# Norms of a diffusion block: squares added in another order, root transposed from one column, transposed root read in PSUM

## The chip, the cores and the metric

The kernel runs on one core of one Trainium2 chip. The metric is the device time of one execution in microseconds (us). The engines are TensorE (PE, with its weight loads PEld), VectorE (DVE), ScalarE (ACT), GpSimd (POOL) and SyncE (SP); DMAs move data between the chip's memory and the on-chip memory SBUF. TensorE writes its results to PSUM, a second on-chip memory of eight banks.

## What is computed

Two layers over 512 latent tokens and 256 context tokens, each token with 1024 features. Layer 0 is attention, layer 1 a Mamba-2 scan (SSD); a gated feed-forward block with a convolution (ConvFFN) follows each. Each sub-layer begins with the same norm:

```python
def rms_norm(x, g):
    xf = x.astype(jnp.float32)
    y = xf * lax.rsqrt(jnp.mean(xf * xf, axis=-1, keepdims=True) + EPS)
    return (y * g.astype(jnp.float32)).astype(x.dtype)

def modulate(x, shift, scale):
    return x * (1 + scale) + shift

for i in range(DEPTH):                       # DEPTH = 2
    h_l = modulate(rms_norm(x, norm_mix_w[i]), mod_l[0], mod_l[1])
    h_c = modulate(rms_norm(ctx, norm_mix_w[i]), mod_c[0], mod_c[1])
    # attention (i = 0) or SSD (i = 1), then x += mod_l[2] * o_l and, for i = 0, ctx += mod_c[2] * o_c
    h_l = modulate(rms_norm(x, norm_ffn_w[i]), mod_l[3], mod_l[4])
    x = x + mod_l[5] * conv_ffn(h_l, ffn_w_up[i], ffn_conv_w[i], ffn_conv_b[i], ffn_w_down[i])
    # the same for ctx when i = 0
```

## The kernel before, in words

Activations lie transposed: a tile is 128 features by up to 512 tokens, and eight tiles (m = 0 to 7) hold the 1024 features. Every large product is made of three matmuls: weights and activations are split into a high part in a shorter number format (fp32r) and a low part, the rest (`wh` and `wl`, `hh` and `hl`). ScalarE casts the high part of a weight, VectorE subtracts to get `wl` (line 87).

A norm needs, for every token, the sum of squares over all features, that is over the partitions of eight tiles. The steps are these:

- `Norm.sq`: as each tile m of the stream x is finished (line 781, VectorE, `X<-ps_d`), ScalarE squares it (line 325). GpSimd adds the squares of tiles 1 to 5 onto that of tile 0. The squares of tiles 6 and 7 are added to each other on VectorE (line 330), and then that sum and the first one (line 332), also on VectorE.
- `rstd_rows`: TensorE sums over the partitions, with the squares as weights and a column of ones (`ss`, line 236); this gives one column per 128 tokens with the tokens on the partitions. VectorE scales it (`rsa`, line 239), ScalarE takes Ln and Exp (line 241, `rsy`), VectorE refines by one Newton step (`rsu`, lines 243 and 244). The last step of it (line 247) writes the root `rb` 128 columns wide, the same value in each, and TensorE transposes it (`rsT`, line 253), so that it lies in PSUM with the tokens along the columns, the same on every partition.
- `Norm.gen`: ScalarE copies `rsT` to SBUF as `rs` (line 345). `modulated` then makes the eight tiles `h`: VectorE multiplies x by the gain and the root (`ht`, line 281), ScalarE adds the shift and writes the high part (line 290, or lines 286 and 287), and VectorE (line 291) or GpSimd (line 288) writes the low part.

`rstd_rows` serves other norms too: the norm `a` ahead of attention, the norm `y` inside the SSD mixer, and the norm `q` of queries and keys, which has two column groups (`cols` of two columns, so c = 2); all others have c = 1.

The class Norm is used three times: f0 (ahead of layer 0's ConvFFN), s (ahead of the SSD mixer) and f1 (ahead of layer 1's ConvFFN). f0 and s have three segments of 256 tokens: the context, then the two halves of the latents; f1 has the two latent halves. While the product ahead of the norm (`down`, tiles `ps_d`, or `ps_wo` for f1) goes on for one segment, the norm of the segment before it runs beside it, one step for every tile m. Behind the product stand the first two output tiles of the next one (`first_tiles`, tiles `ps_first`), segment by segment. They need the `h` of their segment and hide the norm of the segments after it.

PSUM is given out as two double banks (`S`, for `ps_first`) and four single banks:

```python
def Bank(g, name):
    return g.ps.tile([P, 512], F32, tag="B", bufs=4, name=name)
```

`ps_d`, `ps_wo`, `ss` and `rsT` all take one of these four while they live. SBUF tiles such as `rb`, `rs`, `ht` and `sq` come from one pool of equal buffers (`t3`).

The order of instructions on every engine is fixed when the program is built: a planner goes through the program in the order written, with a cost for each instruction, and moves forward what it takes to be ready sooner. On the chip each engine runs its own list in order, and semaphores make it wait for others.

Of the kernel before, what the change touches and what calls it, by code (L numbers as in the profile page):

```python
# [7 lines left out]
P = 128  # L8
# [3 lines left out]
ALU = mybir.AluOpType  # L12
# [55 lines left out]
def t3(g, name, dt=F32, n=T):  # L68
    return g.t3p.tile([P, n], dt, tag="t3", bufs=g.n3, name=name)
# [106 lines left out]
class Fill:  # L176
# [6 lines left out]
    def add(self, gen):  # L183
        self.q.append(gen)
# [17 lines left out]
    def require(self, gen):  # L202
        for _ in gen:
            pass
        if gen in self.q:
            self.q.remove(gen)
# [8 lines left out]
def follow(g, bi):  # L215

    if g.last_act is not None:
        g.tc.add_manual_dep(bi.ins, g.last_act.ins.name, mybir.DependencyInfo(
            mybir.DependencyClass.NoSync, mybir.DependencyReason.DATA), reason="order of tables")
    g.last_act = bi  # L220
# [6 lines left out]
def rstd_rows(g, sq, n, cols, width, name, bank):  # L227

    nc = g.nc
    c = cols.shape[-1]
    nt = n // P
    ps = bank(f"ss{name}")
    for t in range(nt):
        nc.tensor.matmul(ps[:, t * c : (t + 1) * c], sq[:, t * P : (t + 1) * P], cols, start=True, stop=True)
    small = lambda nm: g.p.tile([P, nt * c], F32, tag="rst", bufs=8, name=nm)
    a, y, u = small("rsa"), small("rsy"), small("rsu")
    nc.vector.tensor_scalar(a, ps[:, : nt * c], 1.0 / width, EPS, ALU.mult, ALU.add)

    for f in ((lambda: nc.scalar.activation(y, a, AF.Ln)), (lambda: nc.scalar.activation(y, y, AF.Exp, scale=-0.5))):
        follow(g, f()) if g.tables else f()
    nc.vector.tensor_tensor(u, y, a, ALU.mult)
    nc.vector.scalar_tensor_tensor(u, y, -0.5, u, ALU.mult, ALU.mult)
    rb = t3(g, f"rb{name}", n=n)
    wide = lambda v: v.unsqueeze(2).broadcast_to([P, nt * c, P // c])
    nc.vector.scalar_tensor_tensor(rb.rearrange("p (a b) -> p a b", b=P // c), wide(u), 1.5, wide(y), ALU.add, ALU.mult)
    yield BREAK
    out = []
    for t0 in range(0, nt, 4):  # L250
        pt = bank(f"rsT{name}")
        for t in range(t0, min(nt, t0 + 4)):
            nc.tensor.transpose(pt[:, (t - t0) * P : (t - t0 + 1) * P], rb[:, t * P : (t + 1) * P], g.ident)
        yield (pt, t0 * P, min(n, (t0 + 4) * P))


def parts(x, a=0, b=1 << 30):


    x = x if isinstance(x, list) else [x]  # L260
    out, c = [], 0
    for ap in x:
        n = ap.shape[-1]
        lo, hi = max(a, c), min(b, c + n)
        if lo < hi:
            out.append((ap[:, lo - c : hi - c], lo - a, hi - a))
        c += n
    return out
# [6 lines left out]
def modulated(g, hl, x, rs, a, b, layer, ca, cb, v, m, pool=False):  # L275

    nc = g.nc
    n = b - a
    t = t3(g, "ht", n=n)
    for ap, c0, c1 in parts(x[m], a, b):  # L280
        nc.vector.scalar_tensor_tensor(t[:, c0:c1], ap, g.moda[layer][ca][:, m, v : v + 1], rs[:, c0:c1],  # L281
                                       ALU.mult, ALU.mult)
    bias = g.mod[layer][cb][:, m, v : v + 1]
    hi, lo = (h[:, a:b] for h in hl)
    if pool:
        nc.scalar.activation(t, t, AF.Identity, bias=bias)
        nc.scalar.copy(hi, t)
        nc.gpsimd.tensor_tensor(lo, t, _r(hi), ALU.subtract)
        return
    nc.scalar.activation(hi, t, AF.Identity, bias=bias)  # L290
    nc.vector.scalar_tensor_tensor(lo, t, bias, _r(hi), ALU.add, ALU.subtract)
# [14 lines left out]
def Bank(g, name):  # L306
    return g.ps.tile([P, 512], F32, tag="B", bufs=4, name=name)


class Norm:  # L310
# [8 lines left out]
    def sq(self, seg, x, m):  # L319

        i, a, b = seg
        nc = self.g.nc
        sq = t3(self.g, f"sq{self.name}", n=b - a)
        for ap, c0, c1 in parts(x[i][m], a, b):
            nc.scalar.activation(sq[:, c0:c1], ap, AF.Square)
        if m in (0, 6):
            self.acc[seg, m] = sq
            return
        acc = self.acc[seg, 6 if m == 7 else 0]
        (nc.vector if m == 7 else nc.gpsimd).tensor_tensor(acc, acc, sq, ALU.add)  # L330
        if m == 7:
            nc.vector.tensor_tensor(acc, acc, self.acc[seg, 0], ALU.add)

    def gen(self, seg, x, lag=2):

        i, a, b = seg
        g, nc, n = self.g, self.g.nc, b - a
        for _ in range(lag):
            yield
        rows = rstd_rows(g, self.acc[seg, 6], n, g.ones[:, :1], D, self.name, lambda nm: Bank(g, nm))  # L340
        next(rows)
        for _ in range(lag):
            yield
        rs = t3(g, f"rs{self.name}", n=n)
        nc.scalar.copy(rs, next(rows)[0][:, :n])
        for m in range(KT):
            modulated(g, self.h[i][m], x[i], rs, a, b, *self.a, self.streams[i][1], m,
                      pool=m in ((1, 4) if a else (1, 3, 5, 7)))
            yield
# [30 lines left out]
def attention(g, fill, X, late):  # L380
# [57 lines left out]
    for m in range(KT):  # L438
        sq = t2("sql") if m else acc
        nc.scalar.activation(sq, xs[0][m], AF.Square)  # L440
        if m:
            nc.vector.tensor_tensor(acc, acc, sq, ALU.add)
    norm = rstd_rows(g, acc, L, g.ones[:, :1], D, "a", Bk)
    g.qn8 = g.const.tile([P, 1], F32, name="qn8")
    nc.vector.tensor_scalar(g.qn8, g.par[:, PC["qn"] : PC["qn"] + 1], HD ** -0.5, None, ALU.mult)
# [23 lines left out]
    for m in range(KT):  # L469
# [11 lines left out]
        if m == 3:  # L481
            norm = rstd_rows(g, sqc, C, g.ones[:, :1], D, "a", Bk)
            next(norm)
# [956 lines left out]
```

## Time and profile before

| | |
|---|---|
| median of 3 runs (lowest to highest) | 1893.8 us (1892.28 to 1894.25) |
| the profiled execution | 1893.6 us, span 1891.8 us |
| TensorE busy | 1859.4 us, 98% of the span |
| VectorE busy | 1314.9 us, 70% |
| ScalarE busy | 811.4 us, 43% |
| GpSimd busy | 302.8 us, 16% |
| granted TensorE clock, mean | 0.997 |

A row of a profile view names the line, the engine, the operation, the tiles written and read (`out<-in`), their shape and how often it was. The view of waits gives the engine and the line that waited, behind the arrow the instruction that released it, and the total in us, the number of waits and the longest. The view in order of time gives the start, the duration, the instruction and, in brackets, the idle time of the engine before it. In the view of one line or tile the three numbers are the smallest, median and largest duration in ns. In the view of stretches each engine has its busy time and, in brackets, its instructions; behind the engines stands the granted TensorE clock.

### The profile page before, as it was taken

The numbers are of one execution on the slowest core, as the hardware profiler recorded it, in microseconds if no ns is written. First come the engines' busy times: TensorE is split into PE (matmuls) and PEld (weight loads), VectorE is DVE, ScalarE is ACT, GpSimd is POOL, SyncE is SP. The second block draws the span as 40 slices with busy tenths as digits, with TensorE's granted clock in tenths as the row PEclk, the third lists the DMA queues.
The fourth block names the chain that finished last, engine by engine and source line by source line (L and its number), as shares of the span: only waits on it lengthen the run. The fifth ranks groups of instructions, "written<-read, shape, count | busy, mean of one in ns | idle before, by whom it ended". The sixth has DMA issues, their size and how long they took to land.

```text
span 1891.8 us, 28789 instructions
## 1 busy us (share of the span) xinstructions
PE 1859.4 (98%) x11474; PEld 1548.3 (82%) x11474; DVE 1314.9 (70%) x1950; ACT 811.4 (43%) x1410; POOL 302.8 (16%) x266
## 2 busy tenths in 40 slices
PE   9999999999999999999999999999999999999999
PEld 7866565688888888888888888888887888888887
DVE  6587778687877776444487877777787476565655
ACT  4544443364222222222366676776666252323331
POOL 2231120040000000000041334444333210000000
PEclk9999999999999999999999999999999999999999
DMA  9322341115443553112224323333453222323232
GB/s 342 91 95 62 132 156 37 34 57 190 145 134 131 180 182 123 65 67 68 67 90 125 114 92 116 118 120 126 123 158 106 72 91 100 100 83 107 90 100 89
DMA packets 74070, 211.67 MB, mean 112 GB/s; under 512 B 9040, under 2 KB 14544, under 8 KB 73808
## 3 DMA queue, kind: packets, MB, share of 16 engines
q1 hardware_dynamic: 73936, 209.84, 33.5%
q8 instruction: 90, 1.47, 0.3%
q14 instruction: 44, 0.36, 0.1%
HBM read 198.79 MB, written 6.82 MB: 109 GB/s over the span
## 4 chain that ended last, share of the span: by engine, by line
PE 80%; DVE 11%; issue 3%; DMA 2%; ACT 2%; POOL 1%; SPq 0%; DVEq 0%; POOLq 0%; ACTq 0%
PE ps_up L108 10%; PE ps_up L106 10%; PE ps_up L105 10%; PE ps_d L105 6%; PE ps_d L106 6%; PE ps_d L108 6%; PE ps_in L108 4%; PE ps_in L106 4%; PE ps_in L105 4%; PE ps_o L636 2%; PE ps_s L672 2%; PE ps_st L1030 2%; DVE ht L281 1%; DVE wl L87 1%; PE ps_wo L108 1%
## 5 line engine op out<-in xcount | busy, mean ns | idle before, releaser
L87 DVE TENSOR_TENSOR wl<-wst,wh 128x1024 fp32r<-128x1024 f32 x207 | 260.4, 1258 | 229.3 <-PE ps_up L106 133.0
L85 ACT CAST wh<-wst 128x1024 fp32r<-128x1024 f32 x211 | 221.1, 1049 | 396.4 <-DMA wst<-in_wup 321.5
L106 PE MATMUL ps_up<-hlf,wh 128*128 128x512 f32 (+1 forms) x1008 | 357.0, 354 | 0.0
L108 PE MATMUL ps_up<-hhf,wl 128*128 128x512 f32 (+1 forms) x1008 | 356.8, 354 | 0.0
L105 PE MATMUL ps_up<-hhf,wh 128*128 128x512 f32 x1008 | 356.8, 354 | 0.0
L106 PEld LDWEIGHTS ps_up<-hlf,wh 128*128 128x128 f32 x1008 | 190.7, 189 | 26.3
L105 PEld LDWEIGHTS ps_up<-hhf,wh 128*128 128x128 f32 x1008 | 190.5, 189 | 26.5
L108 PEld LDWEIGHTS ps_up<-hhf,wl 128*128 128x128 f32 x1008 | 190.5, 189 | 26.3
L105 PE MATMUL ps_in<-hhs,wh 128*128 128x512 f32 (+1 forms) x560 | 204.4, 365 | 1.2 <-ACT dt L915 1.2
L106 PE MATMUL ps_in<-hls,wh 128*128 128x512 f32 (+1 forms) x560 | 199.4, 356 | 0.0
L108 PE MATMUL ps_in<-hhs,wl 128*128 128x512 f32 (+1 forms) x560 | 198.7, 355 | 0.0
L105 PE MATMUL ps_d<-hdh,wh 128*128 128x512 f32 (+1 forms) x568 | 193.5, 342 | 0.2 <-ACT hdh L85 0.2
L108 PE MATMUL ps_d<-hdh,wl 128*128 128x512 f32 (+1 forms) x568 | 193.5, 341 | 0.0
L106 PE MATMUL ps_d<-hdl,wh 128*128 128x512 f32 (+1 forms) x568 | 192.9, 340 | 0.3 <-DVE hdl L87 0.3
L781 DVE SCALAR_TENSOR_TENSOR X<-ps_d,mod,X 128x512 f32<-128x512 f32 (+1 forms) x224 | 124.8, 587 | 35.2 <-PE ps_d L108 35.0
L105 PEld LDWEIGHTS ps_in<-hhs,wh 128*128 128x128 f32 x560 | 105.9, 189 | 16.3 <-ACT dt L915 1.4
L106 PEld LDWEIGHTS ps_d<-hdl,wh 128*128 128x128 f32 x568 | 106.7, 188 | 14.8 <-DVE hdl L87 0.7
L108 PEld LDWEIGHTS ps_in<-hhs,wl 128*128 128x128 f32 x560 | 105.8, 189 | 14.8
L108 PEld LDWEIGHTS ps_d<-hdh,wl 128*128 128x128 f32 x568 | 106.7, 188 | 13.1
L105 PEld LDWEIGHTS ps_d<-hdh,wh 128*128 128x128 f32 x568 | 106.3, 188 | 13.6 <-ACT hdh L85 0.7
L106 PEld LDWEIGHTS ps_in<-hls,wh 128*128 128x128 f32 x560 | 106.0, 189 | 13.2
L675 ACT ACTIVATE pr<-ps_s 128x1024 f32<-128x1024 f32 x56 | 57.2, 1022 | 108.8 <-PE ps_s L674 106.5
(344 smaller groups left out, 3682.8 us busy)
## 6 DMA issues: line engine op xcount, KB each, us to landing
wst<-in_wup SPq DMA_DIRECT2D x88, 512.0 KB, 3.3
wada<-in_adaT SPq DMA_DIRECT2D x56, 512.0 KB, 3.3
wst<-in_win SPq DMA_DIRECT2D x48, 512.0 KB, 3.4
wst<-in_wdown SPq DMA_DIRECT2D x44, 512.0 KB, 3.9
E<-ad SPq DMA_DIRECT2D x64, 256.0 KB, 6.4
wada<-in_adaB SPq DMA_DIRECT2D x24, 512.0 KB, 4.0
ec<-ead SPq DMA_DIRECT2D x64, 128.0 KB, 5.1
wst<-in_wout SPq DMA_DIRECT2D x16, 512.0 KB, 3.3
```

Source lines behind the costliest of these rows:

```text
L85: keep(nc.scalar.copy(hi, src))
L87: keep(eng.tensor_tensor(lo, src, _r(hi), ALU.subtract))
L105: mm(out, wh, ah, start=first, stop=False)
L106: mm(out, wh, al, start=False, stop=False)
L108: mm(out, wl, ah, start=False, stop=last)
L281: nc.vector.scalar_tensor_tensor(t[:, c0:c1], ap, g.moda[layer][ca][:, m, v : v + 1], rs[:, c0:c1], ALU.mult, ALU.mult)
L636: nc.tensor.matmul(po[S64[e], :n], v, pr[:, 512 * e + off : 512 * e + off + n], start=first, stop=last)
L672: nc.tensor.matmul(outs[e], kk[e][a][S64[e], k], b[S64[e], q], start=i == 0, stop=False)
L675: nc.scalar.activation(pr, ps, AF.Exp)
L781: nc.vector.scalar_tensor_tensor(ap, o[:, c0:c1], gate[:, m, v : v + 1], ap, ALU.mult, ALU.add)
L1030: nc.tensor.matmul(ps[:, d * 256 : (d + 1) * 256], Bt[:, t * P : (t + 1) * P], xw[d][t], start=t == ts[0], stop=t == ts[-1])
```

## The change

Three edits. In `rstd_rows`, for c = 1, the last Newton step writes one column per 128 tokens, into the small tile `a`; the transposes read this column as a 128x128 operand with a stride of zero. For c = 2 all stays as it was. In `Norm.sq`, for tile 7, the sum of tiles 0 to 5 is added to the square of tile 6 first, and the square of tile 7 last. In `Norm.gen`, `rs` is no longer a copy: `modulated` reads the transposed root in PSUM. The norms a and y keep their copies (lines 461 and 1220); the norm a already reads PSUM for its first tile (line 459).

```diff
-    rb = t3(g, f"rb{name}", n=n)
-    wide = lambda v: v.unsqueeze(2).broadcast_to([P, nt * c, P // c])
-    nc.vector.scalar_tensor_tensor(rb.rearrange("p (a b) -> p a b", b=P // c), wide(u), 1.5, wide(y), ALU.add, ALU.mult)
+    if c == 1:
+        nc.vector.scalar_tensor_tensor(a, u, 1.5, y, ALU.add, ALU.mult)
+        root = lambda t: a[:, t : t + 1].broadcast_to([P, P])
+    else:
+        rb = t3(g, f"rb{name}", n=n)
+        wide = lambda v: v.unsqueeze(2).broadcast_to([P, nt * c, P // c])
+        nc.vector.scalar_tensor_tensor(rb.rearrange("p (a b) -> p a b", b=P // c), wide(u), 1.5, wide(y),
+                                       ALU.add, ALU.mult)
+        root = lambda t: rb[:, t * P : (t + 1) * P]
     yield BREAK
-    out = []
     for t0 in range(0, nt, 4):
         pt = bank(f"rsT{name}")
         for t in range(t0, min(nt, t0 + 4)):
-            nc.tensor.transpose(pt[:, (t - t0) * P : (t - t0 + 1) * P], rb[:, t * P : (t + 1) * P], g.ident)
+            nc.tensor.transpose(pt[:, (t - t0) * P : (t - t0 + 1) * P], root(t), g.ident)
         yield (pt, t0 * P, min(n, (t0 + 4) * P))
...
         acc = self.acc[seg, 6 if m == 7 else 0]
-        (nc.vector if m == 7 else nc.gpsimd).tensor_tensor(acc, acc, sq, ALU.add)
         if m == 7:
             nc.vector.tensor_tensor(acc, acc, self.acc[seg, 0], ALU.add)
+        (nc.vector if m == 7 else nc.gpsimd).tensor_tensor(acc, acc, sq, ALU.add)
...
-        rs = t3(g, f"rs{self.name}", n=n)
-        nc.scalar.copy(rs, next(rows)[0][:, :n])
+        rs = next(rows)[0][:, :n]
```

## The prediction

> **What bounds the kernel now.** I read the busy times on the page first, then the waits of TensorE in the stretches where the norms stand, then the queues of the other engines in those stretches.
>
> ```profile
> PE 1859.4 (98%) x11474; PEld 1548.3 (82%) x11474; DVE 1314.9 (70%) x1950; ACT 811.4 (43%) x1410; POOL 302.8 (16%) x266
> ```
>
> TensorE is the bound over the whole span, so an edit to the norms can only win back places where TensorE stands idle for them. The next rows are TensorE's waits from 392 to 432 us (norm f0), 950 to 990 us (norm s) and 1470 to 1540 us (norm f1); the columns are the total in us, how often, and the longest.
>
> ```profile
> PE rsTf L253 <- DVE rbf L247: 1.0, 3, 0.4
> PE ps_first L106 <- DVE hlf L291: 0.5, 1, 0.5
> PE ps_first L108 <- DVE wl L87: 0.4, 1, 0.4
> ...
> PE rsTs L253 <- DVE rbs L247: 1.0, 3, 0.4
> PE ps_first L106 <- DVE hls L291: 1.0, 2, 0.6
> PE ps_first L108 <- DVE wl L87: 0.6, 1, 0.6
> ...
> PE ps_first L105 <- ACT hhf L290: 1.5, 1, 1.5
> PE ps_first L106 <- POOL hlf L288: 1.2, 1, 1.2
> PE ps_first L105 <- ACT hhf L287: 0.2, 1, 0.2
> PE ssf L236 <- DVE sqf L332: 0.2, 1, 0.2
> ```
>
> They sum to 7.6 us, of which the 1.0 us for wl (a weight's low part) is no work of the norm. So about 6.6 us, 0.35% of the span, is all that a shorter norm can free in waits. There are two kinds: the transpose rsT stands in TensorE's queue before its root is there (2.0 us in six waits), and the first matmuls after the norm lack their tiles h (4.4 us). The rest, 0.2 us, is the row-sum matmul.
>
> The last segment of f0 on VectorE, TensorE and ScalarE shows the chain: additions of squares, row sum, Ln and Exp, root, transpose, copy, ht. The columns are start, duration, instruction, and the idle time before it.
>
> ```profile
> 415.29 0.41 DVE L332 TENSOR_TENSOR sqf<-sqf,sqf 128x256 f32<-128x256 f32 x1
> 415.62 1.66 DVE L281 SCALAR_TENSOR_TENSOR ht<-X,moda,rsf 128x256 f32<-128x256 f32 x4
> 417.20 0.14 DVE L239 TENSOR_SCALAR rsa<-ssf 128x2 f32<-128x2 f32 x1
> 417.27 1.69 DVE L87 TENSOR_TENSOR wl<-wst,wh 128x1024 fp32r<-128x1024 f32 x1
> ...
> 420.70 0.43 DVE L247 SCALAR_TENSOR_TENSOR rbf<-rsu,rsy 128x256 f32<-128x256 f32 x1
> ...
> 422.12 2.07 DVE L281 SCALAR_TENSOR_TENSOR ht<-X,moda,rsf 128x256 f32<-128x256 f32 x5 [0.60 <-ACT rsf L345]
> ...
> 421.18 0.44 PE L253 MATMUL rsTf<-cst,rbf 128*128 128x128 f32 x2 [0.30 <-DVE rbf L247]
> ...
> 421.71 0.37 ACT L345 COPY rsf<-rsTf 128x256 f32<-128x256 f32 x1 [2.49 <-PE rsTf L253]
> ```
>
> VectorE has no rest here but for the 0.60 us in which it waits for the copy. The chain is stretched by what stands in its queue, above all the 1.69 us of wl.
>
> **The change part by part.**
>
> The root. For a norm over one column group (a, f0, s, f1, y) the last step on VectorE shrinks from 256 or 512 columns to one per 128 tokens. The view of that line, and the group of its nearest neighbour, a 128x2 step of the same operation:
>
> ```profile
> L247 DVE SCALAR_TENSOR_TENSOR rbf<-rsu,rsy x5: 424/426/850, 395.4 to 1528.2; 128x256 f32<-128x256 f32 x5
> L244 DVE SCALAR_TENSOR_TENSOR rsu<-rsy,rsu 128x2 f32<-128x2 f32 x3 | 0.5, 162 | 0.1
> ```
>
> So 0.43 becomes 0.16: 0.26 us less, and 0.69 where GpSimd doubled the step to 0.85 (one segment of f0; I take the same for s, whose waits have the same size). The six rsT waits are 0.33 on average, 0.4 at most by this view; four give back 0.26, two 0.4: **1.8 us**.
>
> The transposes. rsT's weights are read from one column with a stride of zero. The trace has such weights once, in line 1141; beside them are ordinary ones:
>
> ```profile
> L1141 PEld LDWEIGHTS ps_end<-acsT,cst x4: 185/189/190, 1015.7 to 1016.1; 128*128 128x128 f32 x4
> L236 PEld LDWEIGHTS ssf<-ones,sqf x20: 186/192/333, 392.7 to 1526.1; 128*128 128x128 f32 x20
> ```
>
> No difference, so nothing. If a column of four bytes did cost double in transpose mode, it would be some 0.14 us in each of 26 loads, mostly under running matmuls: at most 0.3 us a norm.
>
> The copy. In f0 rsT ends at 421.18 + 0.44 = 421.62 and ht starts at 422.12. The 0.50 us between falls to one hand-over, which I put at 0.05 us (copy ends 422.08, ht starts 422.12): 0.45 less on each chain. ScalarE also loses 8 copies of 0.37 us; they stand beside TensorE's work, worth nothing by themselves. In their place ht reads the root from PSUM. The trace has that read once:
>
> ```profile
> L281 DVE SCALAR_TENSOR_TENSOR ht<-X,moda,rsTa x1: 748/748/748, 17.8 to 17.8; 128x512 f32<-128x512 f32 x1
> L281 DVE SCALAR_TENSOR_TENSOR ht<-X,moda,rsl x7: 750/752/2174, 20.8 to 57.3; 128x512 f32<-128x512 f32 x7
> L281 DVE SCALAR_TENSOR_TENSOR ht<-X,moda,rsf x24: 468/474/960, 396.9 to 427.1; 128x256 f32<-128x256 f32 x24
> L281 DVE SCALAR_TENSOR_TENSOR ht<-X,moda,rsf 128x256 f32<-128x256 f32 x24 | 12.0, 532 | 2.2 <-ACT rsf L345 2.2
> L781 DVE SCALAR_TENSOR_TENSOR x<-ps_d,mod,x x176: 472/478/488, 1561.7 to 1888.6; 128x256 f32<-128x256 f32 x176
> ```
>
> 748 ns from PSUM, 750 from SBUF (medians): no loss. The maxima tell more: with two SBUF operands the step goes up to 960 ns (mean 532 in f0, median 474), with one in PSUM (line 781) never over 488. So ht should lose its slow cases and take some 475 ns throughout. I count that only where a slow one stands in a chain that TensorE waits for (below). The far bound is that it stays at its present mean.
>
> [...]
>
> The additions. Before, both additions of the last tile stand behind its square (0.41 for line 332 above, and as much for line 330); after, only one does. The other takes the same time, but can run while ScalarE squares; it waits for GpSimd's addition of tile 5, two tiles earlier, so nothing should pile up behind it on VectorE. In f0 and s the saved 0.41 is lost again in the queue: the row sum rsa, due soon after 415.70, starts at 417.20 behind four ht. So nothing in f0 and s, between 0 and 0.41 each as bounds; in f1 TensorE waits for it (0.2 us, quoted).
>
> The tails. The chain of the last segment is shorter by 0.26 + 0.45 = 0.7 us. In f0 this covers the whole wait of 0.5 for hlf, in s 0.7 of 1.0: **1.2 us**. In f1:
>
> ```profile
> 1528.92 0.38 PE L253 MATMUL rsTf<-cst,rbf 128*128 128x128 f32 x2
> 1530.83 0.39 PE L105 MATMUL ps_first<-hhf,wh 128*128 128x256 f32 x1 [1.52 <-ACT hhf L290]
> ...
> 1517.15 0.97 DVE L281 SCALAR_TENSOR_TENSOR ht<-x,moda,rsf 128x256 f32<-128x256 f32 x1
> ```
>
> rsT did not wait for its root there; it stands behind matmuls. So the copy's 0.45 surely comes off the 1.5, and root and addition (0.67) only if rsT moves forward: I take half, 0.8 in all. The 1.2 for POOL's hlf has the chain of the segment before it, shorter by 0.7, and by 0.49 more where the ht of 0.97 becomes 0.48; three wl of 1.2 stand between, so half, 0.6. With 0.2 for the row sum: **1.6 us**.
>
> After a wait the first matmul is longer (0.39 against 0.28 at 1530.83): some four waits vanish, **0.4 us**.
>
> The bank. The transposed root now occupies one of the four banks B until the last ht of its segment. Of f0:
>
> ```profile
> 399.79 0.47 DVE L781 SCALAR_TENSOR_TENSOR X<-ps_d,mod,X 128x256 f32<-128x256 f32 x1
> ...
> 403.42 0.87 DVE L281 SCALAR_TENSOR_TENSOR ht<-X,moda,rsf 128x256 f32<-128x256 f32 x2
> 404.21 0.47 DVE L781 SCALAR_TENSOR_TENSOR X<-ps_d,mod,X 128x256 f32<-128x256 f32 x1
> ...
> 402.59 0.50 PE L236 MATMUL ssf<-ones,sqf 128*128 128x1 f32 x4
> 402.95 0.36 PE L105 MATMUL ps_first<-hhf,wh 128*128 128x256 f32 x1
> ```
>
> Between 399.79 and 404.21 VectorE empties no ps_d, while TensorE writes three more tiles (about 1.08 us each: nine matmuls 0.12 apart) and the row sum. That is four banks; with the root held until 404.29 it is five. So the third tile and what follows must wait from about 401.5, up to 2.8 us. Cover: from 402.95 TensorE has ps_first matmuls that need no B, and they can come forward. I take 0.3 us for each of f0 and s, **0.6 us lost**, with 0 and 2.8 each as bounds. In f1 fewer tiles use B; nothing.
>
> Nothing else is on the path. In y the transposes start without a wait; in a TensorE waits 1.7 us for the adaLN weights, not for the root:
>
> ```profile
> PE ps_ada L129 <- issue: 1.7, 1, 1.7
> ...
> 1483.84 0.60 PE L253 MATMUL rsTy<-cst,rby 128*128 128x128 f32 x4
> ```
>
> No DMA is added or moved, nothing goes past the queues of SP and GpSimd, and each segment needs two SBUF buffers less (root and copy), which can only bring other tiles forward.
>
> Sum: -1.8 - 1.2 - 1.6 - 0.4 + 0.6 = **-4.4 us**. The profiled execution took 1893.6 us (span 1891.8), the median of the runs is 1893.8; I forecast 1889.4.
>
> **The rivals.**
>
> VectorE's queue eats it. If the order of the queues keeps wl and the ht in front of the chain, the 0.7 us per tail becomes idle time of VectorE. Then the rsT waits stay won (1.8) and little else: about -2, 1891.8. For it: the 1.69 us of wl between rsa and the root. Against it: the copy comes behind wl.
>
> The bank stalls TensorE. If ps_first does not come forward, f0 and s lose 2.8 each instead of 0.3: -4.4 + 5.0, about 1894.4. This is the slower side: beyond 2.5 us a norm the sign turns, beyond 4.4 it is slower than the bound below. The eight ht that read the root are spread over 7.4 us (from 397 to 404.29, by their first start and this row), so a queue that puts more evictions behind them could reach 5 us a norm: 1898.8. Against it: the cover at 402.95.
>
> PSUM operands are slower. If ht from PSUM took the present mean of 532 ns instead of 474, the 24 of three tails would lose 24 x 0.058 = 1.4 us: 1890.8. Against it: 748 against 750, and line 781. [...]
>
> The clock. TensorE ran at half clock once in f1:
>
> ```profile
> 1520.00:1524.00 4.00, 2.63 (x19) 2.12 (x18) 3.96 (x6) 2.38 (x7) 2.33 (x2) 1.00 0.20 51
> 1524.00:1528.00 4.00, 4.00 (x23) 4.00 (x23) 2.30 (x6) 1.76 (x4) 0.00 (x0) 0.57 0.20 80
> ```
>
> The granted clock of 0.57 follows a stretch with TensorE 2.63 of 4.00 us busy. If the shorter wait keeps the clock up, up to 0.43 x 4 = 1.7 us more are won: 1887.7. [...]
>
> **How the numbers follow.** The forecast, with or without the clock's 1.7, has 0.50 (the clock's part 0.12); the queue 0.27; the bank 0.16, half of it slower than the bound; PSUM 0.07. A change of 0.2%, 3.8 us, is what a measurement can tell from none. So faster 0.50; same 0.27 + 0.08 + 0.07 = 0.42; slower 0.08. The forecast alone reaches from 1886.3 to 1890.0. The range with the rivals' cases, leaving out the far bank case and a low tail, is 1885.8 to 1895.0.
>
> **What would show it.** Right: a root of 128x2 near 0.16 us in place of 128x256; no rsT wait over 0.15 us; no copy between rsT and ht; ht between 0.47 and 0.49 us throughout. Wrong: TensorE waiting in front of ps_d for a DVE ht or X around 401 and 960 us (the bank); ht at 0.54 us (PSUM); the waits for hl as long as before with VectorE idle ahead of the root (the queue).

## The result, and the profile after

| | before | after |
|---|---|---|
| median (lowest to highest), 21 runs each | 1894.25 us (1891.56 to 1897.67) | 1888.66 us (1887.21 to 1892.94) |
| ratio after to before, 95% interval | | 0.9975 (0.9968 to 0.9981) |
| the profiled execution, its span | 1893.6 us, 1891.8 us | 1891.03 us, 1889.2 us |
| granted clock in the profiled execution | 0.997 | 0.995 |

The ratio is a gain of 4.7 us (3.6 to 6.1 by its interval, times 1894); the forecast was 4.4. The comparison was made once more, in the third group of experiments, and gave 0.9981 (0.9972 to 0.999); two of its twelve executions of the changed kernel, at a granted clock of 0.75 and 0.77, took 2274 and 2218 us and are left out of every ratio. From that comparison comes a second profile of the changed kernel, which is used below beside the first.

A table over stages says where the gain came from. Each stage runs from the first of the last 216 matmuls `ps_d` ahead of the norm (in f1 the first of all `ps_wo`) to the 48th matmul of the product behind `ps_first` (`ps_up` in f0 and f1, `ps_in` in s), start to start in the traces. So each stage holds the same matmuls in every kernel: 426, 426 and 724. The planner puts some `ps_up` among the last `ps_first`, from none to ten of them by kernel and stage, 0.12 to 0.23 us each; a stage that ended with the last `ps_first` would not compare like with like.

| us | f0 | s | f1 | sum |
|---|---|---|---|---|
| before | 59.59 | 60.68 | 131.31 | 251.58 |
| after | 57.95 | 59.23 | 130.27 | 247.45 |
| after, second profile | 57.85 | 59.20 | 129.35 | 246.40 |

The three norms are 4.1 us shorter in the first profile and 5.2 in the second. That is more than the spans lost (2.6 and 4.5 us): the rest of the program was longer in these two executions, by 1.5 us in the first, where the granted clock was lower. TensorE's waits of the changed kernel in the three stretches that the prediction showed (392 to 432, 950 to 990, 1470 to 1540 us; total, times, longest):

```profile
PE ps_first L106 <- POOL hlf L293: 1.5, 2, 1.1
...
PE ps_first L106 <- POOL hls L293: 1.5, 2, 1.2
PE ps_in L105 <- ACT dt L919: 1.5, 1, 1.5
PE ps_first L105 <- ACT hhs L292: 0.3, 1, 0.3
...
PE ps_first L105 <- ACT hhf L295: 1.1, 1, 1.1
PE rsTf L258 <- DVE rsa L246: 0.9, 1, 0.9
PE ps_first L106 <- DVE hlf L296: 0.7, 1, 0.7
```

The six waits of rsT in f0 and s are gone, and so are those for wl. In their place stands, in both, a wait for a low part from GpSimd; in f1 rsT has a wait of 0.9 that it did not have. (The wait of ps_in is behind the norm; it stood at 1.2 before, just past the stretch.) Without ps_in these are 6.0 us in 8 waits, where the prediction's rows had 7.6 in 15. So the waits themselves gave back 1.6 us only. But a wait costs TensorE more than its length in these traces. Matmuls of 0.28 us follow each other 0.12 us apart; at the wait of 0.46 in f0 before, they start at 426.45, 427.20 and 427.42, which is 0.73 us lost. By the same sum every wait for h or wl in f0 and s costs 0.26 us beyond its length, and every wait of rsT there 0.20. There are seven waits less, so an estimate for this is 1.4 to 1.8 us. About 1 us of the first profile's 4.1 these rows do not place (waits under 0.15 us are not in this view). In the second profile the clock comes on top, for which the next rows are the f1 tail in windows of 4 us, first of the changed kernel, then of its second profile (length, PE, PEld, DVE, ACT, POOL busy with counts, granted clock, DMA share, GB/s):

```profile
1524.00:1528.00 4.00, 2.00 (x13) 1.45 (x12) 3.40 (x9) 1.34 (x4) 0.00 (x0) 0.96 0.00 0
1528.00:1532.00 4.00, 4.00 (x19) 3.57 (x18) 3.93 (x10) 3.54 (x9) 1.64 (x2) 0.61 0.00 0
...
1524.00:1528.00 4.00, 2.17 (x12) 1.67 (x13) 3.40 (x12) 2.29 (x5) 0.06 (x1) 1.00 0.00 0
1528.00:1532.00 4.00, 3.90 (x28) 3.33 (x28) 3.36 (x8) 2.58 (x7) 1.58 (x2) 1.00 0.00 0
```

The same kernel, with waits of 2.7 and 2.8 us in f1: once the window behind them ran at 0.61 with 19 matmuls, once at full clock with 28. f1 is 0.9 us shorter in the second profile. TensorE's busy total over the whole span is 1856.1 us there, 3.3 less than before; in the first profile it is 1860.5, 1.1 more. So the busy total of one profile says little on the change.

What the prediction wanted to see, in rows of the changed kernel (min, median and max in ns; first and last start):

```profile
L286 DVE SCALAR_TENSOR_TENSOR ht<-X,moda,rsTf x24: 467/472/482, 397.1 to 426.4; 128x256 f32<-128x256 f32 x24
L286 DVE SCALAR_TENSOR_TENSOR ht<-X,moda,rsTs x24: 462/473/482, 953.5 to 982.8; 128x256 f32<-128x256 f32 x24
L246 DVE SCALAR_TENSOR_TENSOR rsa<-rsu,rsy x11: 161/162/675, 14.1 to 1525.5; 128x2 f32<-128x2 f32 x9, 128x4 f32<-128x4 f32 x2
L258 PEld LDWEIGHTS rsTq<-cst,rbq x60: 138/141/230, 77.9 to 296.2; 128*128 128x128 f32 x60
L258 PEld LDWEIGHTS rsTf<-cst,rsa x10: 132/133/137, 396.7 to 1525.7; 128*128 128x128 f32 x10
```

ht never takes over 482 ns (960 before). The root takes 0.16 us in ten of its eleven places, and the weights read from one column load no slower than the dense ones of norm q. The eleventh root, 0.68 us, is in the last segment of s. The chain in the last segment of f0, and behind the dots the end of it in s:

```profile
417.18 0.14 DVE L239 TENSOR_SCALAR rsa<-ssf 128x2 f32<-128x2 f32 x1
417.25 1.21 DVE L87 TENSOR_TENSOR wl<-wst,wh 128x1024 fp32r<-128x1024 f32 x1
418.38 0.96 DVE L296 SCALAR_TENSOR_TENSOR hlf<-ht,mod,hhf 128x256 fp32r<-128x256 f32 x1
419.26 0.70 DVE L243 TENSOR_TENSOR rsu<-rsy,rsa 128x2 f32<-128x2 f32 x1
420.70 0.16 DVE L246 SCALAR_TENSOR_TENSOR rsa<-rsu,rsy 128x2 f32<-128x2 f32 x1
421.67 1.26 DVE L286 SCALAR_TENSOR_TENSOR ht<-X,moda,rsTf 128x256 f32<-128x256 f32 x3 [0.41 <-PE rsTf L258]
...
976.39 0.68 DVE L246 SCALAR_TENSOR_TENSOR rsa<-rsu,rsy 128x2 f32<-128x2 f32 x1
...
978.11 1.26 DVE L286 SCALAR_TENSOR_TENSOR ht<-X,moda,rsTs 128x256 f32<-128x256 f32 x3 [0.64 <-PE rsTs L258]
```

From the root's start to the next ht it is 0.97 us in f0 (before: 420.70 to 422.12, 1.42) and 1.72 in s (before 1.42). In the other six segments of the three norms it is 0.69 everywhere, where it was 1.42 to 2.14: root and copy give 0.73 and more there. In these two last segments rsT starts later, behind `ps_first` matmuls in TensorE's queue. From the row sum's `rsa` to ht the last segment is only 0.43 us shorter in f0 (4.92 to 4.49) and 0.31 in s (4.91 to 4.60), and in f1 it is 0.34 longer (3.24 to 3.58). Where TensorE now waits is beside wl, which stands where it stood: a low part of GpSimd's that starts with it, at 417.37, takes 1.69 us, and TensorE waits for that one.

```profile
L293 POOL TENSOR_TENSOR hlf<-ht,hhf x1: 1687/1687/1687, 417.4 to 417.4; 128x256 fp32r<-128x256 f32 x1
...
419.11 0.39 PE L106 MATMUL ps_first<-hlf,wh 128*128 128x256 f32 x1 [1.15 <-POOL hlf L293]
```

The median low part in f0 and f1 takes 0.74 us. In s it is the same: a low part that starts beside wl, at 973.76, takes 1.61 us, and TensorE waits 1.2 us for it.

### The profile page after: what moved, and what is told of

The parts are those of the page before. It is cut to its first block, busy times and chain, and to the rows that moved or that the text cites. A ratio compares the mean times of both kernels' runs of the same rounds, so it can differ in the third digit from the quotient of the medians.

```text
span 1889.2 us, 28788 instructions
## 1 busy us (share of the span) xinstructions
PE 1860.5 (98%) x11474; PEld 1551.5 (82%) x11474; DVE 1306.3 (69%) x1950; ACT 807.6 (43%) x1402; POOL 299.7 (16%) x266
## 4 chain that ended last, share of the span: by engine, by line
PE 78%; DVE 10%; issue 4%; ACT 3%; DMA 2%; POOL 2%; SPq 0%; DVEq 0%; POOLq 0%; ACTq 0%
PE ps_up L105 10%; PE ps_up L106 10%; PE ps_up L108 10%; PE ps_d L105 6%; PE ps_d L106 6%; PE ps_d L108 6%; PE ps_in L106 3%; PE ps_in L108 3%; PE ps_in L105 3%; PE ps_s L676 2%; PE ps_o L640 2%; PE ps_st L1034 1%; DVE Bf L964 1%; DVE xf L964 1%; PE ps_wo L108 1%
## 5 line engine op out<-in xcount | busy, mean ns | idle before, releaser
L106 PE MATMUL ps_up<-hlf,wh 128*128 128x512 f32 x1008 | 357.6, 355 | 0.0
L108 PE MATMUL ps_up<-hhf,wl 128*128 128x512 f32 x1008 | 357.5, 355 | 0.0
```

The source lines that it names most:

```text
L106: mm(out, wh, al, start=False, stop=False)
L108: mm(out, wl, ah, start=False, stop=last)
```

## The experiments

Each kernel was compared with the kernel before on its own chip; ratios have 95% intervals, and 0.001 is 1.9 us. Four kernels of one group share a chip.

**The root alone** (first group, before 1896.93 us):

```diff
+        nc.vector.scalar_tensor_tensor(a, u, 1.5, y, ALU.add, ALU.mult)
+        root = lambda t: a[:, t : t + 1].broadcast_to([P, P])
```

> The root edit alone (one column instead of 256; copy and additions as before). Chain theory (the gain is a shorter chain in front of TensorE): the rsT waits of f0 and s fall from 2.0 us to under 0.5, the tails win 0.26 each, in all -2 to -2.5 us (ratio 0.9988). Contention theory (the gain is ht reading PSUM, free of GpSimd): at most -1 us (0.9995). Order theory (the gain is a planner's new order of the queues, which any edit may change either way): anything from -4 to +2, and the single parts do not add up to the whole.

Measured: 1893.41 us, 0.9975 (0.9962 to 0.9988). The rsT waits are gone from f0 and s in this kernel, too, and waits for X (0.4 us in each) and for GpSimd's low parts (0.9 and 1.1) have come; its profiled f0 is as long as before (59.55), s is 1.9 us longer, with a window of 3.4 us at half clock in it (from 992.1 us), and f1 is 1.1 shorter. So on its chip the narrow root alone is a gain, but its profile does not show the place of it.

**The additions alone:**

```diff
-        (nc.vector if m == 7 else nc.gpsimd).tensor_tensor(acc, acc, sq, ALU.add)
         if m == 7:
             nc.vector.tensor_tensor(acc, acc, self.acc[seg, 0], ALU.add)
+        (nc.vector if m == 7 else nc.gpsimd).tensor_tensor(acc, acc, sq, ALU.add)
```

> The order of additions alone. Chain theory: -0.2 to -0.5 us (0.9998), since in f0 and s the row sum rsa is late in VectorE's queue in any case; only f1's wait for the row sum (0.2 us) goes. Contention theory: 0. Order theory: anything from -3 to +3.

Measured: 1899.13 us, 1.0014 (0.9999 to 1.0028): no gain, and rather a loss. Its profile has the loss in one place, f0, which is 65.63 us long instead of 59.59. First TensorE's wait there, then what GpSimd and VectorE did, then two windows:

```profile
PE ps_first L106 <- POOL hlf L288: 4.4, 2, 4.0
...
422.15 4.86 POOL L288 TENSOR_TENSOR hlf<-ht,hhf 128x256 fp32r<-128x256 f32 x1 [3.96 <-ACT hhf L287]
...
422.44 0.88 DVE L291 SCALAR_TENSOR_TENSOR hlf<-ht,mod,hhf 128x256 fp32r<-128x256 f32 x2
423.23 0.88 DVE L281 SCALAR_TENSOR_TENSOR ht<-X,moda,rsf 128x256 f32<-128x256 f32 x2
424.02 1.27 DVE L291 SCALAR_TENSOR_TENSOR hlf<-ht,mod,hhf 128x256 fp32r<-128x256 f32 x3
425.21 1.22 DVE L87 TENSOR_TENSOR wl<-wst,wh 128x1024 fp32r<-128x1024 f32 x1
...
422.00:426.00 4.00, 1.04 (x8) 0.69 (x6) 4.00 (x10) 2.48 (x7) 3.85 (x1) 0.96 0.00 0
426.00:430.00 4.00, 2.94 (x13) 2.94 (x14) 0.43 (x1) 0.00 (x0) 1.71 (x2) 0.50 0.26 94
```

One subtraction of 128x256 on GpSimd took 4.86 us instead of 0.74, up to 427.01, while VectorE went from one instruction with two SBUF operands to the next without a pause up to 426.43. TensorE waited 4.0 us for it, and the window after it ran at half clock. So what decided in this profile was not the length of the chain but which instructions came to stand side by side.

**The PSUM read alone:**

```diff
-        rs = t3(g, f"rs{self.name}", n=n)
-        nc.scalar.copy(rs, next(rows)[0][:, :n])
+        rs = next(rows)[0][:, :n]
```

> The read of the root in PSUM alone. Chain theory: 0.45 us less in each of three tails, less up to 0.6 us for the bank: about -1.3 us (0.9993); the rsT waits stay at 2.0 us. Contention theory: -3.5 to -4.5 us (0.998), as ht falls from 532 to 475 ns on the mean and GpSimd's subtractions speed up. Bank theory: +1 to +5 us, with TensorE waiting in front of ps_d in f0 and s. Order theory: anything.

Measured: 1890.03 us, 0.9962 (0.9949 to 0.9976). This is the largest part, 7.2 us by the ratio (4.5 to 9.7). Its profile has f0 1.7 us shorter, s 0.4 and f1 2.0, 4.1 in all. Its low parts on GpSimd are shorter, too: the median of `hlf` is 0.75 us (0.92 before).

**Root and PSUM read, additions as before:**

> Root and PSUM read together, additions as before: the whole change without one part. Chain theory: -4 to -4.5 us, all but 0.2 to 0.5 of the whole change's 4.7 (0.9978). Contention theory: nearly all of it too. Order theory: differs from the whole change by more than 1.5 us, one way or the other.

Measured: 1887.79 us, 0.995 (0.9931 to 0.9969). The two gains add up within their intervals (0.0025 + 0.0038). The three norms are 245.96 us in its profile, 0.4 and 1.5 less than with the whole change (246.40 and 247.45), so a gain by the additions is not to be seen. The ratio is better than that of the whole change (0.9975, 0.9981), but most of this lies in the kernel before: its median is 1896.93 us in this group, 1894.25 and 1893.33 beside the whole change. The two kernels themselves took 1887.79 against 1888.66 and 1889.39. No chip had both side by side, and why the kernel before is 2.7 to 3.6 us slower in this group than there is not known; so the gains of this group may be too large when they are carried to another chip.

**The bank held, nothing else** (second group, before 1895.67 us): the copy stays, and only the last ht reads the bank, so the bank is occupied as in the changed kernel and the chain is as long as before.

```diff
+        pt = next(rows)[0][:, :n]
         rs = t3(g, f"rs{self.name}", n=n)
-        nc.scalar.copy(rs, next(rows)[0][:, :n])
+        nc.scalar.copy(rs, pt)
...
-            modulated(g, self.h[i][m], x[i], rs, a, b, ...
+            modulated(g, self.h[i][m], x[i], pt if m == KT - 1 else rs, a, b, ...
```

> The kernel before with one difference: the last of the eight ht of a segment reads the root in PSUM, the other seven the copy as before, so that the bank stays taken to the segment's last ht and nothing is gained. My term: 0.3 us lost in each of f0 and s, +0.6 us (1.0003), with ps_first matmuls moved ahead of the third ps_d tile. Bank theory: up to 2.8 us a norm, +2 to +5.6 us (1.001 to 1.003), with TensorE waits in front of ps_d.

Measured: 1895.18 us, 0.9993 (0.998 to 1.0006). The held bank can be seen, in f0 and in s, where the row sum now waits for the last ht:

```profile
PE ssf L236 <- DVE ht L281: 0.4, 1, 0.4
...
PE sss L236 <- DVE ht L281: 0.7, 1, 0.7
```

In the time it does not show: the interval goes from 3.8 us faster to 1.1 slower, which rules out a loss of 2 us or more but not one of 0.6. The changed kernel has no such wait over 0.15 us.

**The copy behind tile 0:** the changed kernel, in which tile 0 reads PSUM and tiles 1 to 7 a copy, so the first ht starts as early as in the changed kernel and the bank is free soon.

```diff
+            if m == 1:
+                rs = t3(g, f"rs{self.name}", n=n)
+                nc.scalar.copy(rs, pt)
-            modulated(g, self.h[i][m], x[i], rs, a, b, ...
+            modulated(g, self.h[i][m], x[i], rs if m else pt, a, b, ...
```

> The whole change, but only the first ht of a segment reads PSUM; behind it ScalarE copies the root and the other seven read the copy. The chain to the first ht is as short as in the whole change, the bank is free early, but ht has two SBUF operands again. Chain theory: -4 to -4.7 us as the whole change (0.9976), ht up to 0.96 us again without much harm. Contention theory: most of the gain is lost, -1 to -2 us (0.9993). Bank theory: better than the whole change, -5 to -6.

Measured: 1900.06 us, 1.0024 (1.0008 to 1.0041), slower than before. In its profile s is 66.06 us long (60.68 before). The wait and GpSimd's low parts there:

```profile
PE ps_first L106 <- POOL hls L293: 5.1, 2, 4.2
...
L293 POOL TENSOR_TENSOR hls<-ht,hhs x10: 731/834/4602, 956.2 to 986.5; 128x256 fp32r<-128x256 f32 x10
```

It is the picture of the additions alone: ht with two SBUF operands in a run without pauses, one low part of 4.60 us, a wait of 4.2. So this kernel says nothing on the bank; it shows what ht in SBUF can do. In all kernels here whose eight ht all read PSUM, no low part of GpSimd's took over 1.82 us; with ht in SBUF the longest was 1.46 to 4.86, by kernel.

**The order kept:** the changed kernel, and in it the casts of weights that the program states behind a norm's root stay behind its Exp on ScalarE, and their low parts wl behind the root on VectorE. No semaphore is added; only the planner may not move them forward past these two.

```diff
+    if behind and lo_engine == "dve":
+        for x, first in ((i, behind[0]), (j, behind[1])):      # i: cast, j: wl; first: Exp, root
+            g.tc.add_manual_dep(x.ins, first.ins.name, ...)    # order on the engine alone
```

> The whole change, and weights' casts (ScalarE) and low parts wl (VectorE) that the program states behind a norm's root may not be moved ahead of its Exp and its root. In the profile after, the last segment of f1 has a cast of 1.03 us between Ln and Exp and a wl of 1.23 us ahead of the root steps, f0 and s a wl of 1.2 us. Chain theory: f1's chain gets 2 us shorter, its waits of 0.9 and 1.1 us go; f0 and s win up to 1 us each less what the later wl costs: -2 to -4 us beyond the whole change (0.9960). Rival: TensorE then waits for wl instead (first ps_up matmuls), no gain or +1 us.

Measured: 1885.59 us, 0.9945 (0.9926 to 0.9963). The three norms take 243.70 us, 3.8 and 2.7 less than in the two profiles of the changed kernel. All of that is in f0 (56.50 us) and s (56.77). Two things changed in the rows. One is the chain, best seen in f1's last segment. First ScalarE and VectorE of the changed kernel, then VectorE of this one:

```profile
1522.58 0.16 DVE L239 TENSOR_SCALAR rsa<-ssf 128x2 f32<-128x2 f32 x1 [0.76 <-PE ssf L236]
1522.88 1.03 ACT L85 CAST wh<-wst 128x1024 fp32r<-128x1024 f32 x1
1523.82 0.20 ACT L241 ACTIVATE rsy<-rsy 128x2 f32<-128x2 f32 x1
1523.95 1.23 DVE L87 TENSOR_TENSOR wl<-wst,wh 128x1024 fp32r<-128x1024 f32 x1 [1.21 <-ACT wh L85]
1525.47 0.16 DVE L246 SCALAR_TENSOR_TENSOR rsa<-rsu,rsy 128x2 f32<-128x2 f32 x1
...
1522.80 0.16 DVE L243 TENSOR_SCALAR rsa<-ssf 128x2 f32<-128x2 f32 x1 [0.76 <-PE ssf L240]
1523.46 0.16 DVE L249 TENSOR_TENSOR rsu<-rsy,rsa 128x2 f32<-128x2 f32 x1 [0.51 <-ACT rsy L245]
1523.85 0.16 DVE L252 SCALAR_TENSOR_TENSOR rsa<-rsu,rsy 128x2 f32<-128x2 f32 x1
```

In the changed kernel a cast of 1.03 stands between Ln and Exp, and VectorE waits for it in order to make a wl of 1.23 ahead of the root: 2.89 us from row sum to root. With the order kept it is 1.05, and rsT no longer waits in f1 (the row sum ahead of it waits 0.9 for the additions now). Yet f1 as a stage is no shorter: 130.43 us, and 130.27 in the first profile of the changed kernel, each with one window of 3.4 us at half clock. The other thing is GpSimd's low parts, of the changed kernel and of this one:

```profile
L293 POOL TENSOR_TENSOR hlf<-ht,hhf x16: 737/742/1687, 400.7 to 1530.8; 128x256 fp32r<-128x256 f32 x16
...
L301 POOL TENSOR_TENSOR hlf<-ht,hhf x16: 733/744/846, 403.1 to 1528.4; 128x256 fp32r<-128x256 f32 x16
```

With ht in PSUM and wl elsewhere, none of them takes over 0.85 us, and TensorE's waits for them fall from 1.5 to 0.3 us in f0 and in s, where the gain is.

**Fewer low parts on GpSimd:** the kernel with the order kept, with tiles 1 and 4 on GpSimd in every segment (before: tiles 1, 3, 5, 7 in the context and in the first half of the latents).

```diff
-                      pool=m in ((1, 4) if a else (1, 3, 5, 7)))
+                      pool=m in (1, 4))
```

> As the kernel before this one, and GpSimd makes the low part of tiles 1 and 4 only, in every segment (before: 1, 3, 5, 7 in the context and the first latent half). In the profile after, TensorE waits 1.5 us for GpSimd's low parts in f0 and 1.5 in s; a subtraction takes VectorE 0.47 us and GpSimd 0.74 to 1.6. Chain theory: these waits go, but VectorE has two more subtractions in each segment: -1 to -2 us beyond the kernel before this one. Rival: VectorE is full in these stretches and TensorE waits for it instead: 0 to +2 us.

Measured: 1885.58 us, 0.9946 (0.9931 to 0.9961): no more to be had there. VectorE takes over what GpSimd loses, and rsT waits 0.4 in f0 and 1.0 in s for the root.

**PSUM read with the chain as long as before** (third group, before 1893.33 us): the copy is made in place, in the bank, and ht reads the bank.

```diff
-        rs = t3(g, f"rs{self.name}", n=n)
-        nc.scalar.copy(rs, next(rows)[0][:, :n])
+        rs = next(rows)[0][:, :n]
+        nc.scalar.copy(rs, rs)
```

> The kernel before, with ScalarE's copy of the transposed root made in place, in its PSUM bank, and ht reading that bank (the bank is held, ht has a PSUM operand, and the leg of the copy, some 0.45 us in each of f0, s and f1, is still in the chain). The PSUM read alone, without the copy, gave 0.9962. Theory 'shorter chain': the gain came from the leg taken out, so this kernel gives back most of it: 0.9985 to 1.0005, and the wait for the root comes back in each tail. Theory 'contention': the gain came from ht no longer meeting GpSimd in SBUF (24 ht of f0 at a mean of 473 ns, not 532, is 1.4 us there): ht stays at 460 to 490 ns everywhere and the kernel keeps at least half of the gain, 0.996 to 0.998.

Measured: 1892.4 us, 0.9998 (0.9989 to 1.0008). The row of ht, and the waits of f0:

```profile
L281 DVE SCALAR_TENSOR_TENSOR ht<-X,moda,rsTf x24: 465/472/480, 397.1 to 426.5; 128x256 f32<-128x256 f32 x24
...
PE ps_first L105 <- ACT hhf L290: 1.0, 1, 1.0
PE ps_first L106 <- POOL hlf L288: 0.8, 2, 0.6
PE rsTf L253 <- DVE rbf L247: 0.3, 1, 0.3
```

ht is as short and as even as in the changed kernel, and the gain is gone; from `rsa` to ht the last segment takes 5.00 us in f0 and in s, as before (4.92 and 4.91). So the 60 ns that each ht gained are worth nothing that can be measured; the gain of the PSUM read is the copy's leg in the chain. What comes with a shorter chain comes with it: the median low part of `hlf` on GpSimd is 0.93 us here (0.92 before), and 0.75 with the copy gone. How much of the gain goes through these was not separated.

**The whole change again:** the changed kernel itself.

> The whole change, as the reference for the next two on the same chip. Root and PSUM read without the additions edit gave 0.995 elsewhere, the whole change 0.9975. Theory 'the additions edit does nothing or harms': 0.996 to 0.998 again, above the kernel with the order kept and no additions edit. Theory 'chips differ': near 0.995, as root and PSUM read gave.

Measured: 1889.39 us, 0.9981 (0.9972 to 0.999).

**The order kept, additions as before:** root, PSUM read and order, without the third edit.

> Root and PSUM read, additions as in the kernel before, and the casts and low parts of the weights that the program states behind a norm's root kept behind it on ScalarE and VectorE. With the additions edit the same order gave 0.9945. Theory 'the additions edit costs VectorE its wait for GpSimd' (1.8 us idle in f0's three squares): this one is faster by 0.5 to 1.5 us, 0.9935 to 0.9945. Theory 'it takes an addition off the chain as meant': slower by 0.5 to 1.2 us, 0.9948 to 0.9955. Theory 'neither, TensorE does not wait for it': the same within 0.5 us.

Measured: 1884.44 us, 0.9954 (0.9942 to 0.9966), and 0.0027 below the whole change on this chip. The norms take 243.00 us, 243.70 with the edit of the additions; the difference in time between the two (0.9954 and 0.9945, on two chips) is within the intervals. The third theory, that TensorE does not wait for it, fits. The waits of TensorE in f0 and in f1:

```profile
PE ps_first L110 <- POOL hlf L302: 0.3, 1, 0.3
...
PE ssf L240 <- DVE sqf L346: 0.4, 2, 0.3
PE ps_first L110 <- POOL hlf L302: 0.3, 1, 0.3
```

This is the fastest kernel measured, 1884.44 us.

**The order alone**, on the kernel before:

> The kernel before with that order alone: wide root, copy and additions as before. Theory 'the queue took the place of what the change removed': before the change the low parts stood in the same queue but the chain was longer for other reasons, so the order alone brings under 1.5 us, 0.9992 to 1.0005, and its gain shows only with the shorter chain. Theory 'the queue is a cost of its own in f0, s and f1': it brings the same 3 to 4 us as on the changed kernel, 0.998 to 0.9985.

Measured: 1891.55 us, 0.9994 (0.9983 to 1.0006). Nothing that can be measured, as the first theory had it. f0's waits show what took the place: wl is behind the root in the last segment now, and `rsa` to ht is 3.73 us there (4.92 before), but TensorE still waits 0.7 us for the wide root, and now 1.4 us for GpSimd's low parts.

```profile
PE ps_first L110 <- POOL hlf L296: 1.4, 3, 0.8
PE rsTf L261 <- DVE rbf L253: 0.7, 2, 0.4
PE ps_first L112 <- DVE wl L87: 0.4, 1, 0.4
```

## Why the prediction was right, and where not

The time came out at 1888.66 for 1889.4, and the sum of -4.4 stands beside -4.1 and -5.2 in the norms of the two profiles. The way was as forecast: a shorter chain from the squares to h frees TensorE. That the sum came so close is in part luck, as single terms were off both ways.

- The root's waits, -1.8: right in size. All six waits (2.0 us) are gone, the root takes 0.16 but for one of 0.68. The line "no rsT wait over 0.15 us" failed in f1: the new wait of 0.9 is the rival of VectorE's queue, with the cast and wl between row sum and root. The prediction argued this rival from f0's rows only.
- The copy's leg, 0.45 on each chain: right where nothing else stood in the way (root and copy together gave 0.73 and more in six segments of eight), and the copy in place takes the gain away. The PSUM read alone brought 4.5 to 9.7 us by its ratio and 4.1 in its profile; an estimate of its share from the prediction's terms is about 1 us (0.8 in the tails, 0.7 in f1, less 0.6 for the bank).
- The tails of f0 and s, -1.2: this step failed. It took 0.7 off the chain of the last segment, against the waits for VectorE's hlf and hls. That chain got shorter by 0.43 and 0.31 only, and those waits went all the same; but GpSimd's low parts were late next, at 1.5 us in each norm, because the first of them runs beside wl (1.69 and 1.61 us). With wl moved behind the root these waits are 0.3. What went besides were the two wl waits, 1.0 us, which the prediction called no work of the norm.
- f1, -1.6: measured -1.0 and -2.0, the difference by whether a window of half clock came behind its waits. The clock as a rival was right in kind, but it is a matter of the single execution rather than of the kernel, and the two profiles differ by 0.9 us there, not 1.7.
- The first matmul after a wait, -0.4 for four waits at 0.11: undersized about four times. Seven waits went, at 0.20 to 0.26 each, 1.4 to 1.8 us.
- The additions, nothing in f0 and s: no gain is to be seen there. The reason given was wrong: "nothing should pile up behind it on VectorE" does not hold. VectorE now idles for GpSimd's addition, in f0:

```profile
L336 DVE TENSOR_TENSOR sqf<-sqf,sqf 128x256 f32<-128x256 f32 x3 | 1.9, 626 | 1.8 <-POOL sqf L337 1.8
```

  With the order kept, the kernel with these 1.8 us has norms of 243.70 us and the one without the edit 243.00, so the idle time costs little, if anything. Taken alone, the edit rather costs, through the low part of 4.86 us.
- The bank, +0.6: not seen. No ps_d and no row sum waits over 0.15 us for it in the changed kernel; with the longer chain the row sum did wait, 0.4 and 0.7 us. The rival that would have been slower is out. That ps_first is its cover fits, but was not tried.
- PSUM operand: a mean of 473 ns in f0 and never over 482, not the mean of 532, so this rival is out.

What stays open: why the kernel before is about 3 us slower in the first group than beside the whole change, and so how large root and PSUM read are on one and the same chip; how much the order adds to these two edits (by the profiles 245.96 to 243.00 us; no chip had both); and where in its profile the narrow root alone has its gain. That one long low part makes the additions alone and the copy behind tile 0 slow is read from one profile of each; no kernel took this low part away by itself.

## What to carry to other kernels

Before counting what a shorter chain gives, look at what will be late next, on every engine, and at what the fixed queues place between its steps: here a cast and a subtraction for a later product, which the planner had moved into the chain, cost about as much as the whole change brought (0.0030 and 0.0027 of the time, the first across two chips, the second with the additions as before), but only once the chain was short. Beside an unbroken run of VectorE instructions with two SBUF operands a subtraction on GpSimd took 4.86 and 4.60 us here instead of 0.74, so see what stands beside such a run. Price a wait of TensorE with what it costs beyond its length, some 0.26 us here, and, if it lasts a few us, with a possible window at half clock: behind the waits of 2.7 us in f1 one of 3.4 us came, behind those of 2.8 us in the other execution none. And when stages of two kernels are compared, count the matmuls in them: the planner may have moved some across the border.

## What was not expected of the hardware

- GpSimd beside VectorE: a subtraction of 128x256 took 0.74 us by its median in the changed kernel, 1.61 and 1.69 beside one wl, and 4.86 us in the additions alone beside an unbroken run of VectorE instructions with two SBUF operands. In the other direction, beside these subtractions in f0 of the changed kernel, a VectorE step of 0.47 us took 0.96, and a 128x2 step of 0.16 us took 0.70.
- The clock: inside these programs it fell to half for 3.4 us (three times in the profile before, twice in the one after) or twice that (6.8 us, twice in the one after). In the norms TensorE had been idle for 1.4 to 2.9 of the 3.4 us ahead of such a stretch, never for all of it. Not every stretch has such waits ahead of it: TensorE was idle for 0.55 of the 3.41 us ahead of the one at 121.4 us in the changed kernel, and in the order alone it was busy for 3.40 of the 3.41 us ahead of the one at 169.4 us. The waits of f1 in the changed kernel were followed by one in one execution and not in the other. Executions of one kernel differ along with it: over 211 executions, 1.5 us for each 0.001 of the mean granted clock, which accounts for 56% of the variance (least squares, each kernel around its own mean on its chip).
- A wait of TensorE cost more than its length: 0.26 us more ahead of a 128x256 matmul and 0.20 ahead of rsT, start to start, in f0 and s.
- Weights read from one column with a stride of zero loaded as fast as dense ones: 133 against 141 ns by the medians of rsTf and rsTq in the changed kernel.
